# Low parts of one weight pair in four by an accumulating DMA, and pairs used one step later, in the feed-forward parts of a decoder layer

## The chip, the cores and the metric

The kernel runs on one core of a Trainium2 chip. The metric is device time in microseconds (us) for one execution. The engines are named as the profile names them: PE multiplies matrices (PEld is its weight load), DVE works on vectors, ACT on activations and copies, POOL is the general-purpose engine, which also issues DMAs whose descriptors software makes, and SP issues the weight loads. All of them run their own instruction queues in order and wait for each other by semaphores.

## What is computed

One hybrid decoder layer on `x` of 256 rows by 2048 columns, float32: a half-step SwiGLU feed-forward part with layer norm, a mixer (differential attention beside an RWKV-7 recurrence, with layer norm), and a second half-step feed-forward part with layer norm.

```python
def swiglu(x, w_gate, w_up, w_down):
    return (jax.nn.silu(x @ w_gate) * (x @ w_up)) @ w_down

x = layer_norm(alpha * x + 0.5 * swiglu(x, ffn1_w_gate, ffn1_w_up, ffn1_w_down), ln1_g, ln1_b)
p = x @ w_in
...                                   # attention and RWKV-7 on the columns of p
x = layer_norm(alpha * x + concat(o_attn, o_rwkv) @ w_out, ln2_g, ln2_b)
x = layer_norm(alpha * x + 0.5 * swiglu(x, ffn2_w_gate, ffn2_w_up, ffn2_w_down), ln3_g, ln3_b)
```

`D_MODEL` is 2048 and `D_FF` 5632, so each feed-forward part multiplies the 256 rows by two 2048x5632 matrices and one 5632x2048 matrix.

## The kernel before

**Three products for one.** PE multiplies in a rounded float32 form (`fp32r`). To keep float32 accuracy, each operand is split into a rounded high part and a low part, which is the original minus the high part. A product is then high x high, plus high x low, plus low x high: lines 113, 114 and 115. The names say which part an operand is: `wh` and `wl` for weights, `xh` and `xl` for the layer's input, `hh` (both parts) for the hidden activations.

**The weight stream.** All big products go through one object, `Stream`. Its method `block` runs over one block of up to 512 output columns and takes the inner dimension in pairs of 128-row tiles. One pair is one step, counted by `self.step` through the whole kernel. A step does this:

1. SP issues the load of 512 KB from HBM into a tile `raw` (line 134). There are three `raw` buffers (`NRAW`).
2. ACT copies `raw` into `wh`, which rounds it (line 137).
3. DVE subtracts `wh` from `raw` into `wl` (line 138).
4. `mm` issues the six matmuls of the pair for the first 128 rows of `x` (`tt` 0).
5. The pair is put on the list `pend`. Once that holds more than `LAG` pairs, the oldest one has its six matmuls for the second 128 rows (`tt` 1), and its `wh` and `wl` buffers are given back when those are done.

In a feed-forward part there are seven buffers for `wh` and `wl` (`NW`), taken in turn by `self.slot`, and `LAG` is 4: the pair of step s is used for the first rows in step s and for the second rows in step s + 4. In the mixer these are five and 2.

**The feed-forward part.** `ffn` runs in two halves of 6 and 5 blocks of hidden columns. For each block it runs a gate block and an up block of 8 steps each, then ACT takes the silu (line 222), DVE multiplies (line 227), PE transposes (line 230), and ACT and DVE split the result into two parts (lines 240 and 241). Then four down blocks of 12 or 10 steps add into `y`. A feed-forward part thus has 264 steps; the mixer has 136, so the first part is steps 1 to 264 and the second 401 to 664. At the end of each part `ln_tail` makes the layer norm, first for the first 128 rows, then for the second ones (lines 185 to 196), and `flush` issues the second-row matmuls that are still on `pend`.

**What else is on the queues.** POOL does a one-column copy ahead of each reload of the residual (line 262), one small operation of each layer norm (line 189), and the DMAs of the gains and biases (lines 207 and 208) and of the mixer's small tables (lines 289 to 319). ACT issues the DMAs of the residual. A planner of the framework orders each engine's instructions and places the waits; the `raw` tiles and the PSUM tiles are handed out from pools by it.

Of the kernel before, what the change touches and what calls it, by code (L numbers as in the profile page):

```python
# [10 lines left out]
F32 = mybir.dt.float32  # L11
F32R = mybir.dt.float32r
AF = mybir.ActivationFunctionType
ALU = mybir.AluOpType
AX = mybir.AxisListType

P = 128
# [10 lines left out]
LAMBDA_INIT = 0.8 - 0.6 * math.exp(-0.3 * 0)  # L28
LDEC = math.exp(-0.5)
SCALE = 64 ** -0.5  # L30
LAG = {"ffn": 4, "mix": 2}
NW = {"ffn": 7, "mix": 5}
NRAW = 3
BANKS = {"tr": ("at", 2), "sm": ("sm", 2), "pr": ("pr", 1), "at": ("at", 2)}
# [4 lines left out]
def build(tc, A, out):  # L39
# [15 lines left out]
    def nm(s):  # L55
        uid[0] += 1
        return f"{s}_{uid[0]}"

    V, SC, G, T = nc.vector, nc.scalar, nc.gpsimd, nc.tensor
# [29 lines left out]
    class Stream:  # L89
        def __init__(self):  # L90
            self.pend = []
            self.acc = {}
            self.bg = []
            self.credit = {}
            self.hooks = {}
            self.step = 0
            self.slot = 0
# [21 lines left out]
        def block(self, src, c0, w, ks, lhs, done):  # L119
            blk = dict(ks=ks, w=w, lhs=lhs, done=done)  # L120
            for ki in range(0, len(ks), 2):
                for f in self.hooks.get(self.step, ()):
                    f()
                self.step += 1
                n = 2
                r0 = ks[ki][0]
                raw = wp.tile([P, n, NB], F32, tag="raw", name=nm("raw"), bufs=NRAW)
                pool = wp if self.slot < NW["mix"] else self.pool
                wh, wl = (pool.tile([P, n, NB], F32R, tag=f"{t}{self.slot}", name=nm(t)) for t in ("wh", "wl"))
                self.slot = (self.slot + 1) % NW[self.name]  # L130
                g = 1 if self.step == 1 else n
                for k in range(0, n, g):
                    c = slice(k, k + g)
                    nc.sync.dma_start(out=raw[:, c, :w], in_=src[(r0 + k) * P:(r0 + k + g) * P, c0:c0 + w].rearrange("(k p) n -> p k n", p=P))
                for k in range(0, n, g):
                    c = slice(k, k + g)
                    SC.copy(out=wh[:, c, :w], in_=raw[:, c, :w])  # L137
                    V.tensor_tensor(out=wl[:, c, :w], in0=raw[:, c, :w], in1=wh[:, c, :w].bitcast(F32), op=ALU.subtract)  # L138
                st = (blk, ki, n, wh, wl)
                self.mm(st, 0)  # L140
                self.pend.append(st)
                if len(self.pend) > max(0, min(LAG[self.name], self.step // 4 - 1)):
                    self.mm(self.pend.pop(0), 1)
                self.run_bg()

        def flush(self):
            while self.pend:
                self.mm(self.pend.pop(0), 1)

# [813 lines left out]
```

## Time and profile before

| | |
|---|---|
| time, median of 2 runs (lowest, highest) | 2006.34 us (2005.94, 2006.73) |
| span of the profiled execution, first to last instruction | 2006.8 us |
| instructions | 24924 |
| PE busy | 1972.1 us, 98% of the span |
| weight loads of PE busy | 1618.6 us, 81% |
| DVE busy | 1145.7 us, 57% |
| ACT busy | 885.0 us, 44% |
| POOL busy | 34.2 us, 2% |
| moved by DMA | 373.35 MB, 186 GB/s on average |

The profiled execution is one of its own; its span stands within 0.05% of both timed runs. An engine's busy time is the union of its instructions, so a matmul row of 0.39 us overlaps the next one, since matmuls are pipelined. In a row of the order of time stand the start, the duration, engine, line, operation, output and input, and in brackets how long the engine had been idle and what ended that. In a row of the costliest groups stand busy time and mean duration in ns, and then the idle time before. In a row of the waits stand the total wait, the number and the longest.

### The profile page before, as it was taken

The numbers are of one execution on the slowest core, as the hardware profiler recorded it, in microseconds if no ns is written. First come the engines' busy times: TensorE is split into PE (matmuls) and PEld (weight loads), VectorE is DVE, ScalarE is ACT, GpSimd is POOL, SyncE is SP. The second block draws the span as 40 slices with busy tenths as digits, with TensorE's granted clock in tenths as the row PEclk, the third lists the DMA queues.
The fourth block names the chain that finished last, engine by engine and source line by source line (L and its number), as shares of the span: only waits on it lengthen the run. The fifth ranks groups of instructions, "written<-read, shape, count | busy, mean of one in ns | idle before, by whom it ended". The sixth has DMA issues, their size and how long they took to land.

```text
span 2006.8 us, 24924 instructions
## 1 busy us (share of the span) xinstructions
PE 1972.1 (98%) x9671; PEld 1618.6 (81%) x9671; DVE 1145.7 (57%) x1419; ACT 885.0 (44%) x1096; POOL 34.2 (2%) x68
## 2 busy tenths in 40 slices
PE   9999999999999999999999989999999999999997
PEld 7888888888888878878778777788888888888886
DVE  5555554445545566776668777745554544454555
ACT  5444443344444335645565444444444334444432
POOL 0200000000000000000000010000000000000000
PEclk9999999999999999999999989899999999999999
DMA  7766666667666656555445635666666666766663
GB/s 243 220 188 189 187 191 206 211 192 230 190 188 189 195 167 192 155 160 171 137 123 147 187 117 171 210 200 189 189 188 190 206 211 191 230 190 188 190 195 128
DMA packets 202008, 373.35 MB, mean 186 GB/s; under 512 B 22826, under 2 KB 24944, under 8 KB 201120
## 3 DMA queue, kind: packets, MB, share of 16 engines
q1 hardware_dynamic: 182928, 350.53, 57.8%
q10 hardware_dynamic: 17440, 14.29, 2.5%
q0 software_dynamic: 1520, 6.93, 1.0%
q8 instruction: 76, 1.25, 0.3%
q14 instruction: 44, 0.36, 0.0%
HBM read 364.10 MB, written 7.60 MB: 185 GB/s over the span
## 4 chain that ended last, share of the span: by engine, by line
PE 91%; DVE 4%; DMA 2%; ACT 1%; issue 1%; ACTq 0%; POOL 0%; DVEq 0%
PE acc L113 28%; PE acc L115 28%; PE acc L114 28%; DVE wl L138 1%; DMA raw<-in_ffn_w_gate_dram 1%; PE tr L230 1%; ACT wh L137 1%; DVE y L193 1%; DVE y L194 1%; PE sm L556 0%; PE tr L353 0%; DMA raw<-in_ffn_w_up_dram 0%; PE pr L498 0%; PE at L775 0%; PE tr L75 0%
## 5 line engine op out<-in xcount | busy, mean ns | idle before, releaser
L138 DVE TENSOR_TENSOR wl<-raw,wh 128x1024 fp32r<-128x1024 f32 (+1 forms) x665 | 807.9, 1217 | 649.1 <-ACT wh L137 648.4
L137 ACT CAST wh<-raw 128x1024 fp32r<-128x1024 f32 (+1 forms) x665 | 694.9, 1047 | 832.7 <-PE acc L115 728.3
L115 PE MATMUL acc<-wh,xl 128*128 128x512 f32 (+1 forms) x1952 | 740.6, 391 | 0.5 <-DVE xl L82 0.5
L114 PE MATMUL acc<-wl,xh 128*128 128x512 f32 (+1 forms) x1952 | 735.4, 392 | 3.9 <-DVE wl L138 3.9
L113 PE MATMUL acc<-wh,xh 128*128 128x512 f32 (+1 forms) x1952 | 728.1, 392 | 0.3 <-ACT xh L81 0.2
L114 PEld LDWEIGHTS acc<-wl,xh 128*128 128x128 f32 x1952 | 368.0, 189 | 80.0 <-DVE wl L138 5.2
L113 PEld LDWEIGHTS acc<-wh,xh 128*128 128x128 f32 x1952 | 368.2, 189 | 79.1 <-issue 3.0
L115 PEld LDWEIGHTS acc<-wh,xl 128*128 128x128 f32 x1952 | 367.8, 188 | 77.0 <-issue 2.3
L115 PE MATMUL acc<-wh,hh 128*128 128x512 f32 x704 | 254.5, 390 | 0.0
L114 PE MATMUL acc<-wl,hh 128*128 128x512 f32 x704 | 253.6, 389 | 0.0
L113 PE MATMUL acc<-wh,hh 128*128 128x512 f32 x704 | 252.6, 389 | 0.0
L114 PEld LDWEIGHTS acc<-wl,hh 128*128 128x128 f32 x704 | 132.1, 188 | 27.6
L115 PEld LDWEIGHTS acc<-wh,hh 128*128 128x128 f32 x704 | 132.2, 188 | 27.4
L113 PEld LDWEIGHTS acc<-wh,hh 128*128 128x128 f32 x704 | 132.1, 188 | 27.4
L241 DVE TENSOR_TENSOR hh<-tr,hh 128x512 fp32r<-128x512 f32 x44 | 30.4, 691 | 64.2 <-ACT hh L240 64.2
L240 ACT CAST hh<-tr 128x512 fp32r<-128x512 f32 x44 | 25.8, 586 | 91.2 <-PE tr L230 91.2
L227 DVE SCALAR_TENSOR_TENSOR h<-sg,acc 128x512 f32<-128x512 f32 x44 | 30.2, 687 | 34.9 <-PE acc L115 34.9
L222 ACT ACTIVATE sg<-acc 128x512 f32<-128x512 f32 x44 | 26.3, 598 | 42.9 <-PE acc L115 42.9
L230 PEld LDWEIGHTS tr<-ident,h 128*128 128x128 f32 x176 | 21.7, 140 | 6.3 <-DVE h L227 0.7
L230 PE MATMUL tr<-ident,h 128*128 128x128 f32 x176 | 26.4, 272 | 0.3 <-DVE h L227 0.3
L584 DVE TENSOR_TENSOR itmp<-U,Y 64x31 f32<-64x31 f32 (+15 forms) x62 | 20.5, 331 | 7.3 <-DMA U<-dU 5.9
L586 DVE TENSOR_TENSOR Y<-Y,itmp 64x31 f32<-64x31 f32 (+15 forms) x62 | 20.6, 332 | 1.4
(239 smaller groups left out, 746.8 us busy)
## 6 DMA issues: line engine op xcount, KB each, us to landing
raw<-in_ffn_w_up_dram SPq DMA_DIRECT2D x176, 512.0 KB, 3.8
raw<-in_ffn_w_down_dram SPq DMA_DIRECT2D x176, 512.0 KB, 4.2
raw<-in_ffn_w_gate_dram SPq DMA_DIRECT2D x175, 512.0 KB, 3.9
raw<-in_w_in_dram SPq DMA_DIRECT2D x96, 512.0 KB, 3.7
raw<-in_w_out_dram SPq DMA_DIRECT2D x32, 512.0 KB, 4.2
xs<-y ACTq DMA_DIRECT2D x16, 256.0 KB, 3.1
rc<-xs ACTq DMA_DIRECT2D x16, 256.0 KB, 4.3
lng<-in_ln_g_dram POOLq DMA_DIRECT2D x3, 1024.0 KB, 6.5
```

Source lines behind the costliest of these rows:

```text
L113: T.matmul(a, hi, wh[:, j, :w], start=(ki + j == 0), stop=False)
L114: T.matmul(a, hi, wl[:, j, :w], start=False, stop=False)
L115: T.matmul(a, lo, wh[:, j, :w], start=False, stop=(ki + j == last))
L137: SC.copy(out=wh[:, c, :w], in_=raw[:, c, :w])
L138: V.tensor_tensor(out=wl[:, c, :w], in0=raw[:, c, :w], in1=wh[:, c, :w].bitcast(F32), op=ALU.subtract)
L222: SC.activation(out=s, in_=acc, func=AF.Silu)
L227: V.scalar_tensor_tensor(out=h, in0=sg[tt], scalar=0.5, in1=acc, op0=ALU.mult, op1=ALU.mult)
L230: T.transpose(tr[:, i, :], h[:, i * P:(i + 1) * P], ident)
L240: SC.copy(out=hi, in_=tr)
L241: V.tensor_tensor(out=lo, in0=tr, in1=hi.bitcast(F32), op=ALU.subtract)
L584: V.tensor_tensor(out=tv, in0=U[:, 0:j, j:j + 1].to_broadcast([64, j, 32 - j]), in1=Y[:, j:j + 1, j:32].to_broadcast([64, j, 32 - j]), op= ...
L586: V.tensor_tensor(out=Y[:, 0:j, j:32], in0=Y[:, 0:j, j:32], in1=tv, op=ALU.add)
```

## The change

For the steps of a feed-forward part after step 16, those whose number leaves the remainder 3 or 7 modulo 8 get their low part in another way: ACT writes the negated, rounded tile into `wl` (an activation `Copy` with scale -1), and then a DMA issued by POOL adds the raw tile onto it in place. At remainder 3 the DMA reads the weights from HBM a second time, at remainder 7 it reads the `raw` tile in SBUF. The other steps keep the subtraction on DVE.

In the same steps a pair is kept back on a list `held` for one step, so that its matmuls for the first rows are issued after the next pair's conversions have been; `LAG` for the feed-forward part goes from 4 to 3. `flush` and the steps that don't hold pairs empty the list first.

```diff
-LAG = {"ffn": 4, "mix": 2}
+LAG = {"ffn": 3, "mix": 2}
...
             self.pend = []
+            self.held = []
...
                     SC.copy(out=wh[:, c, :w], in_=raw[:, c, :w])
-                    V.tensor_tensor(out=wl[:, c, :w], in0=raw[:, c, :w], in1=wh[:, c, :w].bitcast(F32), op=ALU.subtract)
+                    src_c = src[(r0 + k) * P:(r0 + k + g) * P, c0:c0 + w].rearrange("(k p) n -> p k n", p=P)
+                    how = self.step % 8 if self.name == "ffn" and self.step > 16 else 0
+                    if how in (3, 7):
+                        SC.activation(out=wl[:, c, :w], in_=raw[:, c, :w], func=AF.Copy, scale=-1.0)
+                        G.dma_start(out=wl[:, c, :w], in_=src_c if how == 3 else raw[:, c, :w], accum_op=ALU.add)
+                    else:
+                        V.tensor_tensor(out=wl[:, c, :w], in0=raw[:, c, :w], in1=wh[:, c, :w].bitcast(F32), op=ALU.subtract)
                 st = (blk, ki, n, wh, wl)
+                if self.name == "ffn" and self.step > 16:
+                    self.held.append(st)
+                    if len(self.held) < 2:
+                        continue
+                    st = self.held.pop(0)
+                else:
+                    self.unhold()
                 self.mm(st, 0)
...
+        def unhold(self):
+            while self.held:
+                st = self.held.pop(0)
+                self.mm(st, 0)
+                self.pend.append(st)
+
         def flush(self):
+            self.unhold()
             while self.pend:
                 self.mm(self.pend.pop(0), 1)
```

## The prediction, made before the change was run

> **What bounds the kernel now.** I read the head of the page first, then busy time by stretch, then the waits, then the order of time inside one feed-forward (FFN) stretch. "Step" is one weight pair (two 128x512 tiles).
>
> ```profile
> span 2006.8 us, 24924 instructions
> PE 1972.1 (98%) x9671; PEld 1618.6 (81%) x9671; DVE 1145.7 (57%) x1419; ACT 885.0 (44%) x1096; POOL 34.2 (2%) x68
> ...
> 58.00:735.00 677.00, 677.00 (x3029) 560.31 (x3027) 342.54 (x316) 279.77 (x288) 13.44 (x32) 1.00 0.65 197
> 735.00:760.00 25.00, 20.30 (x115) 18.05 (x114) 23.33 (x41) 9.79 (x16) 2.04 (x2) 0.86 0.52 165
> 1235.00:1275.00 40.00, 36.17 (x156) 28.83 (x155) 36.49 (x53) 13.32 (x17) 2.00 (x2) 0.87 0.61 191
> 1275.00:1985.00 710.00, 710.00 (x3175) 587.62 (x3174) 360.46 (x323) 295.48 (x304) 2.82 (x12) 1.00 0.65 196
> 1985.00:2006.00 21.00, 9.85 (x44) 7.83 (x42) 14.13 (x24) 0.00 (x0) 2.01 (x2) 0.86 0.30 101
> ```
>
> The columns of a stretch are its length, then busy time of PE, weight loads, DVE, ACT, POOL, then granted clock, DMA share and GB/s. In the two FFN stretches (677 and 710 us) PE is busy for all of it, at clock 1.00. The whole span leaves 2006.8 - 1972.1 = 34.7 us without PE, none of it in these two.
>
> Is that busy time PE's own pace, or something that slows it? The order of time answers:
>
> ```profile
> 404.39 1.05 ACT L137 CAST wh<-raw 128x1024 fp32r<-128x1024 f32 x1 [1.67 <-PE acc L115]
> 407.11 1.05 ACT L137 CAST wh<-raw 128x1024 fp32r<-128x1024 f32 x1 [1.67 <-PE acc L115]
> ...
> 420.71 1.05 ACT L137 CAST wh<-raw 128x1024 fp32r<-128x1024 f32 x1 [1.67 <-PE acc L115]
> ```
> ```profile
> 405.47 1.23 DVE L138 TENSOR_TENSOR wl<-raw,wh 128x1024 fp32r<-128x1024 f32 x1 [0.56 <-ACT wh L137]
> 408.19 1.22 DVE L138 TENSOR_TENSOR wl<-raw,wh 128x1024 fp32r<-128x1024 f32 x1 [1.49 <-ACT wh L137]
> ```
> ```profile
> 404.64 0.39 PE L114 MATMUL acc<-wl,hh 128*128 128x512 f32 x1
> 404.87 0.39 PE L115 MATMUL acc<-wh,hh 128*128 128x512 f32 x1
> 405.09 0.39 PE L113 MATMUL acc<-wh,hh 128*128 128x512 f32 x1
> 405.32 0.39 PE L114 MATMUL acc<-wl,hh 128*128 128x512 f32 x1
> 405.55 0.39 PE L114 MATMUL acc<-wl,xh 128*128 128x512 f32 x1
> 405.77 0.39 PE L115 MATMUL acc<-wh,xl 128*128 128x512 f32 x1
> ```
>
> A step takes (420.71 - 404.39) / 6 = 2.72 us; with 12 matmuls that is 0.227 us each. Matmul starts stand 0.22 to 0.23 us apart while ACT alone works (404.64 to 405.32) and while DVE does (405.55 to 405.77), so easing DVE can't quicken them. ACT idles 1.67 us before each conversion, and what ends the wait is PE giving back a weight buffer: the feed waits for PE.
>
> ```profile
> ACT wh L137 <- PE acc L115: 728.3, 472, 8.2
> ...
> PEld acc L114 <- DVE wl L138: 5.2, 4, 2.5
> ...
> PE acc L114 <- DVE wl L138: 3.9, 3, 2.2
> ```
> ```profile
> SPq L134 <- DVE wl L138: 1451.2, 594, 29.8
> ```
>
> PE waited for a low part 5.2 and 3.9 us in the whole run. SP, which issues the loads, waits for line 138 to give back a raw buffer. **So nothing in the FFNs can be gained; the question is whether the new chain still fits.**
>
> **The change part by part.**
>
> *Counting.* Steps 17 to 264 (first FFN) and 401 to 664 (second; the mixer has 136 steps) are concerned. Remainders 3 and 7 modulo 8 occur 31 times each in the first and 33 in the second: 128 pairs, in 64 periods of 8 steps (21.8 us each).
>
> *Removed:* 128 subtractions of 1.22 us = 156 us of DVE. Off the path by the waits above: worth nothing.
>
> *Added on ACT:* 128 negated copies. The trace has none; the nearest row is line 137, same engine and shape, 1.05 us (134 us in all, ACT 885 to about 1,020). The activation of line 222 against the cast of line 240, both 512 wide, bounds the form:
>
> ```profile
> L240 ACT CAST hh<-tr 128x512 fp32r<-128x512 f32 x44 | 25.8, 586 | 91.2 <-PE tr L230 91.2
> ...
> L222 ACT ACTIVATE sg<-acc 128x512 f32<-128x512 f32 x44 | 26.3, 598 | 42.9 <-PE acc L115 42.9
> ```
>
> 12 ns in 586, so 1.05 to 1.08. Behind it on ACT stands the next conversion, which has 1.67 us of idle time; that hides it once, with 1.05 us of ACT per 2.72 us step.
>
> *Added on POOL and the DMA engines:* 128 accumulating DMAs of 512 KB. No row shows one. The nearest:
>
> ```profile
> q1 hardware_dynamic: 182928, 350.53, 57.8%
> ...
> raw<-in_ffn_w_up_dram SPq DMA_DIRECT2D x176, 512.0 KB, 3.8
> ...
> lng<-in_ln_g_dram POOLq DMA_DIRECT2D x3, 1024.0 KB, 6.5
> lnb<-in_ln_b_dram POOLq DMA_DIRECT2D x3, 1024.0 KB, 9.1
> ```
> ```profile
> 454.48 0.53 POOL L207 DMA_DIRECT2D lng<-in_ln_g_dram  x1 [0.20 <-POOL lnb L206]
> ```
>
> 350.53 MB take 57.8% of 2006.8 us, so 302 GB/s while busy, and 512 KB (0.524 MB) is 1.74 us of all 16 engines. A plain load lands in 3.8 us, so about 2.06 us of it is fixed. An accumulation must read its destination as well as its source: 2.06 + 2 x 1.74 = 5.5 us alone, 7.3 with one load interleaved. The layer-norm gain, 1 MB on the same software queue beside the loads, took 6.5. I take L = 6.4 us from issue to landing, near that row. Bounds: 3.8 (costs as a load) and 9.1 (the second of two such transfers). The DMA engines have room: 8 loads and 2 accumulations are 14 + 7 = 21 of 21.8 us at the busy rate, tight but below one.
>
> The Trainium skill weighs against this number. "DMA: Bandwidth & Descriptors", section "Anatomy of one DMA — SWDGE (gpsimd) path", gives 2.0 us plus bytes over 436 GB/s; its price for the gain's 1 MB is 4.4 us, the row says 6.5, so I keep the row. "Collectives: The Full Stack", section "The bandwidth ceiling: the fold count and why AG ≠ RS ≠ AR", says an adding DMA costs its second source read and not the add; no run here shows it yet. By the formula with two reads L would be 4.4 and the change would be hidden.
>
> *Used one later, lag 3 instead of 4.* Let T = 2.72 and 0 be the moment a weight buffer comes free. Before, the pair is needed 2T = 5.4 us later, and casting plus subtracting takes 1.05 + 1.23 + gaps = 2.4. After, the second half of the rows still runs at the same place (held 1 + lag 3), so the buffer frees at the same place, but the first use is at 3T = 8.16, the low part at about 8.4 (second matmul). Ordinary pairs gain cover. An accumulated pair needs 1.05 + 1.05 + 0.15 (gaps) + L = 2.25 + L = 8.65: late by **0.25 us**.
>
> *Raw buffers, the larger term.* There are three. For remainder 7 the source is the raw tile itself, so it is held to the landing at 8.65 instead of 2.4. I assume that the pool hands on the buffer that is free first: the load three steps on takes the next pair's buffer (free at 5.1), the one four steps on, itself an accumulated pair (remainder 3), takes the held one. SP issues in order, so later loads queue behind it. It is issued at 8.75, lands at 12.55 instead of 10.9, is cast and negated by 14.75, and its low part lands 14.85 + 6.4 = 21.25. PE wants it at 7T + 0.23 = 19.3, plus the first 0.25: late by **1.7**. Together 1.9 us a period (2L - 10.9 in general); the remainder-3 pair gives its raw tile back after the negation, so the chain recovers before the next period.
>
> 64 x 1.9 = **122 us**.
>
> *One-offs.* In the flush, the held pair's first half now runs after one second half fewer, 6 matmuls = 1.4 us less PE work to hide the first rows' layer norm. At the end DVE goes from it to the second rows' without a gap:
>
> ```profile
> 1992.59 2.73 DVE L194 SCALAR_TENSOR_TENSOR y<-y,rs,lnb 128x512 f32<-128x512 f32 x4
> 1995.24 0.68 DVE L266 TENSOR_TENSOR y<-y,acc 128x512 f32<-128x512 f32 x1
> ```
>
> so +1.4 us there and +1.4 at the first FFN's end. Gains, biases and the mixer's small tables go through the same POOL queue; an accumulation behind one gain and bias (9.1 us for both) is some 3 us later still, twice: about 6. On the other side at most the 4.7 + 3.8 us that PE idles in the two layer-norm stretches could go; I count nothing. Sum of one-offs: about +8.
>
> 122 + 8 = 130 on 2006.8, the profiled span, which is the median of the timed runs (2006.34) within 0.03%: **2135 us**.
>
> **The rivals.**
>
> *Hidden (not slower).* L of 5.4 or less makes 2L - 10.9 negative: the one-step hold covers the accumulation, and only the one-offs stay, 2007 + 3 to 8, about **2013**. For it: 5.5 us alone, and PE's order, in which first-half and second-half matmuls (hh at 405.32, xh at 405.55) are interleaved, so a planner that foresees a late low part may put other matmuls ahead. Against: the 6.5 us row, taken under just these loads. Also 65% of the DMA time in these stretches is already taken. The formula of the Trainium skill's DMA page, 4.4 us by the section named above, speaks for this rival, and the same row against it.
>
> *Strict rotation.* If the load three steps on waits for the held buffer itself, the next load is issued right behind it and lands 1.5 us later: 2L - 9.4 = 3.4 us a period, 218 + 8: **2233**. The pool's order isn't visible in the trace, where subtractions release in order either way.
>
> *The accumulation is slow.* At L = 8 to 9.1 a period loses 5.1 to 7.3 us: **2340 to 2480**, and stalls so long would cost clock too (0.86 in the stretches with layer norms). It decides from about twice the 3.8 us of a load.
>
> **How the numbers follow.** Forecast (stall of 1 to 2.5 us a period, 2080 to 2175) 0.38; hidden 0.34; rotation 0.16; slow accumulation 0.11; faster by more than 2% (40 us, which is also about what a measurement of this kernel can tell from no change) 0.01, since PE without work is only 34.7 us in all. The range reaches from hidden, 2003, to above rotation, 2310, and leaves out most of the slow case. Within 2% takes hidden whole: 0.34; slower 0.65.
>
> **What would show it.** In the profile after: PE waiting for a DMA on the low part at line 114 for 100 us or more; the accumulating issues landing near 6.4 us; SP waiting for the same DMAs; DVE down by 156 us, ACT up by 134. The forecast is wrong if they land under 5.5 us, or over 8, or if SP's raw loads get slower than 4.5 us beside them, and if the FFN stretches stay at full PE busy time.

## The result, and the profile after

The changed kernel takes **2252.62 us** (median of 2 runs, 2245.59 to 2259.65) against 2006.34: a ratio of 1.1226, interval 1.1143 to 1.1309. The forecast was 2135, the range 2003 to 2310. The profiled execution took 2245.59, its span is 2243.8.

Head of the page after, its queues, three groups, and its DMA issues (the last column is us to landing), with some lines between left out:

```profile
span 2243.8 us, 25241 instructions
PE 2044.5 (91%) x9671; PEld 1650.6 (74%) x9671; DVE 986.9 (44%) x1291; ACT 1003.5 (45%) x1224; POOL 169.8 (8%) x196
...
q1 hardware_dynamic: 182928, 350.53, 48.9%
q0 software_dynamic: 28144, 74.04, 17.3%
...
L142 ACT ACTIVATE wl<-raw 128x1024 fp32r<-128x1024 f32 x128 | 135.8, 1061 | 189.6 <-PE acc L115 156.8
L143 POOL DMA_DIRECT2D wl<-raw x64 | 58.2, 910 | 728.4 <-ACT wl L142 727.6
L143 POOL DMA_DIRECT2D wl<-in_ffn_w_gate_dram x21 | 25.6, 1218 | 304.5 <-ACT wl L142 304.5
...
raw<-in_ffn_w_up_dram SPq DMA_DIRECT2D x176, 512.0 KB, 4.6
raw<-in_ffn_w_down_dram SPq DMA_DIRECT2D x176, 512.0 KB, 5.0
wl<-raw POOLq DMA_DIRECT2D x64, 512.0 KB, 4.6
wl<-in_ffn_w_down_dram POOLq DMA_DIRECT2D x22, 512.0 KB, 9.7
wl<-in_ffn_w_gate_dram POOLq DMA_DIRECT2D x21, 512.0 KB, 8.9
```

The span grew by 237 us. PE without work went from 34.7 to 2243.8 - 2044.5 = 199.3 us (+164.6), PE busy time from 1972.1 to 2044.5 (+72.4). The landings fall into two kinds in this kernel: 4.6 us where the source is the raw tile in SBUF, 9 to 10 us where it is HBM. SP's own loads of the FFN weights are slower too, 3.8 to 4.6 us for `up`.

Granted clock over the run, from the view of the cores; first the kernel before, then after:

```profile
core 0: 2006.8 us, clock 0.990
```
```profile
core 0: 2243.8 us, clock 0.963
```

2243.8 x 0.037 = 83 us against 2006.8 x 0.010 = 20. So about 63 of the 72 us of extra busy time are clock, not work.

Busy time by stretch after (columns as in the prediction), of most of the two FFNs:

```profile
58.00:700.00 642.00, 583.74 (x2483) 471.90 (x2483) 216.06 (x204) 279.56 (x292) 66.26 (x82) 0.96 0.76 214
1450.00:2200.00 750.00, 678.93 (x2884) 549.68 (x2883) 253.36 (x235) 320.40 (x332) 64.13 (x68) 0.96 0.74 210
```

Before, PE was busy for every microsecond of the FFN stretches, at clock 1.00. Now it lacks 58 of 642 and 71 of 750 us, at 0.96. What it waits for, from the waits after (total us, times, longest), and below them a row of SP's own waits:

```profile
PE acc L115 <- DMA wl<-in_ffn_w_down_dram: 67.6, 22, 5.6
...
PE acc L115 <- DMA wl<-in_ffn_w_up_dram: 43.4, 20, 3.3
PE acc L115 <- DMA wl<-in_ffn_w_gate_dram: 39.0, 18, 4.5
```
```profile
SPq L135 <- DMA wl<-raw: 402.4, 61, 10.2
```

(Line 115 is the low-part matmul, line 114 before.) These three rows are 150.0 us in 60 waits, 2.5 us each, all for a pair whose accumulation reads HBM (remainder 3; there are 64 periods). For an accumulation from the raw tile PE waited 1.3 us in the whole run, in two waits. Yet SP waited 402 us for just those. The chain of work that ended last, in order of time (start, us; short pieces left out), shows how one becomes the other:

```profile
1620.91 4.72 DMA wl<-raw
1625.69 0.37 SPq L135
1626.17 4.73 DMA raw<-in_ffn_w_gate_dram
1631.00 1.07 ACT wl L142
...
1632.52 9.49 DMA wl<-in_ffn_w_gate_dram
1642.06 0.50 PE acc L115
...
1643.61 0.43 PE acc L114
```

The remainder-7 accumulation lands at 1625.63; only then does SP issue the next two loads. The second is the remainder-3 pair's: landed at 1630.90, negated, accumulated from HBM, and PE starts the moment that lands. Its idle time then is 2.55 us:

```profile
1642.06 0.50 PE L115 MATMUL acc<-wl,xh 128*128 128x512 f32 x1 [2.55 <-DMA wl<-in_ffn_w_gate_dram]
```

Afterwards, from 1643.6 to 1646.4, a matmul takes 0.43 us instead of 0.23. Two stretches around it, columns as above (the granted clock is the third from the end):

```profile
1632.00:1642.00 10.00, 7.50 (x35) 5.86 (x34) 3.74 (x4) 3.77 (x6) 1.21 (x1) 1.00 0.87 237
...
1644.00:1647.00 3.00, 3.00 (x10) 2.35 (x9) 0.92 (x2) 1.22 (x2) 0.00 (x0) 0.56 0.49 138
```

### The profile page after: what moved, and what is told of

It reads as the page before. It is cut to its first block, busy times and chain, and to the rows that moved or that the text cites. A ratio compares the mean times of both kernels' runs of the same rounds, so it can differ in the third digit from the quotient of the medians.

```text
span 2243.8 us, 25241 instructions
## 1 busy us (share of the span) xinstructions
PE 2044.5 (91%) x9671; PEld 1650.6 (74%) x9671; DVE 986.9 (44%) x1291; ACT 1003.5 (45%) x1224; POOL 169.8 (8%) x196
## 3 DMA queue, kind: packets, MB, share of 16 engines
q1 hardware_dynamic: 182928, 350.53, 48.9%
q0 software_dynamic: 28144, 74.04, 17.3%
## 5 line engine op out<-in xcount | busy, mean ns | idle before, releaser
L145 DVE TENSOR_TENSOR wl<-raw,wh 128x1024 fp32r<-128x1024 f32 (+2 forms) x537 | 651.2, 1215 | 1058.1 <-ACT wh L138 1057.6
L115 PE MATMUL acc<-wl,xh 128*128 128x512 f32 (+1 forms) x1952 | 776.2, 401 | 87.2 <-DMA wl<-in_ffn_w_up_dram 43.4
L114 PE MATMUL acc<-wh,xh 128*128 128x512 f32 (+1 forms) x1952 | 764.8, 399 | 12.7 <-ACT xh L81 9.8
L116 PE MATMUL acc<-wh,xl 128*128 128x512 f32 (+1 forms) x1952 | 770.3, 399 | 0.5 <-DVE xl L82 0.5
L115 PE MATMUL acc<-wl,hh 128*128 128x512 f32 x704 | 283.4, 406 | 67.6 <-DMA wl<-in_ffn_w_down_dram 67.6
L116 PE MATMUL acc<-wh,hh 128*128 128x512 f32 x704 | 280.0, 405 | 0.0
L114 PE MATMUL acc<-wh,hh 128*128 128x512 f32 x704 | 276.0, 400 | 0.0
L142 ACT ACTIVATE wl<-raw 128x1024 fp32r<-128x1024 f32 x128 | 135.8, 1061 | 189.6 <-PE acc L115 156.8
L143 POOL DMA_DIRECT2D wl<-raw x64 | 58.2, 910 | 728.4 <-ACT wl L142 727.6
L143 POOL DMA_DIRECT2D wl<-in_ffn_w_gate_dram x21 | 25.6, 1218 | 304.5 <-ACT wl L142 304.5
L143 POOL DMA_DIRECT2D wl<-in_ffn_w_down_dram x22 | 26.6, 1210 | 204.5 <-ACT wl L142 203.1
```

Source lines behind the costliest of these rows:

```text
L114: T.matmul(a, hi, wh[:, j, :w], start=(ki + j == 0), stop=False)
L115: T.matmul(a, hi, wl[:, j, :w], start=False, stop=False)
L116: T.matmul(a, lo, wh[:, j, :w], start=False, stop=(ki + j == last))
L142: SC.activation(out=wl[:, c, :w], in_=raw[:, c, :w], func=AF.Copy, scale=-1.0)
L143: G.dma_start(out=wl[:, c, :w], in_=src_c if how == 3 else raw[:, c, :w], accum_op=ALU.add)
```

## The experiments

Edits are against the changed kernel unless said. Ratios are to the kernel before in the same session (2007.1 to 2009.0 us there).

### No accumulation, only the later use

```diff
-                    if how in (3, 7):
+                    if how in ():
```

> Pairs used one later and lag 3, but every low part by the subtraction: no negated copy, no accumulating DMA. Two theories of the 237 us that the changed kernel lost. HOLD: the raw tile that the remainder-7 DMA keeps delays the load for the remainder-3 pair, and that delay is most of the loss. LANDING: the DMA that reads HBM lands 8.9 to 9.7 us after its issue (4.6 for the one that reads SBUF), which is more than the cover by itself. Both expect 2007 + 1.4 + 1.4 for the shorter flush, 2008 to 2010. Over 2030 would mean that the order of use itself costs time, and both would be short of a cause.

**2022.56 us, 1.0076 (1.0059 to 1.0093)**: a miss, some 15 us rather than a few. The stretches of this kernel, and of the kernel before below them:

```profile
58.00:735.00 677.00, 677.00 (x3027) 560.28 (x3027) 340.66 (x316) 280.61 (x287) 13.24 (x32) 1.00 0.65 196
735.00:1290.00 555.00, 527.63 (x3210) 423.07 (x3209) 400.89 (x724) 282.54 (x474) 15.27 (x16) 0.97 0.52 155
```
```profile
735.00:1275.00 540.00, 522.12 (x3194) 419.85 (x3193) 396.50 (x721) 280.74 (x473) 15.27 (x16) 0.97 0.53 158
```

The first FFN is as full of PE work as before. The loss lies in the stretch behind it, where PE lacks 27.4 us instead of 17.9. So the later use costs nothing where it acts, and something at its end.

### The later use in the second FFN alone

```diff
-                    if how in (3, 7):
+                    if how in ():
...
-                if self.name == "ffn" and self.step > 16:
+                if self.name == "ffn" and self.step > 400:
...
-                if len(self.pend) > max(0, min(LAG[self.name], self.step // 4 - 1)):
+                if len(self.pend) > max(0, min(LAG[self.name] + (self.name == "ffn" and self.step <= 400), self.step // 4 - 1)):
```

> Pairs used one later and lag 3 in the second feed-forward part alone, no accumulation. The run with both parts so took 15 us more than the kernel before, with PE busy for all of the two feed-forward stretches. If that comes from the first part's end, through another order in the mixer behind it: 2007 to 2011 here. If the order of use costs in each part: 2013 to 2017.

**2010.2 us, 1.0011 (1.0001 to 1.0021).**

The middle stretch is again that of before: PE works 521.64 of its 540 us, after 522.12. The 15 us hang on the first FFN's end and on how the mixer's work is planned behind it; which instruction there is late wasn't traced further.

### One of the two accumulations alone

Remainder 3, from HBM:

```diff
-                    if how in (3, 7):
+                    if how == 3:
```

> Only remainder 3 (HBM source) is accumulated, 64 pairs; remainder 7 by the subtraction, so no raw tile is held. LANDING: 2.25 + 9.4 us against 8.4 us of cover is 3.3 us late, 64 times: 209 us, with slow clock behind the waits up to 250: 2200 to 2260. HOLD: without the late load at most a third of the loss is left: under 2090.

**2147.99 us, 1.0700 (1.0669 to 1.0731)**, between what the two theories had. From its waits, then its DMA issues:

```profile
PE acc L115 <- DMA wl<-in_ffn_w_down_dram: 52.2, 22, 3.1
```
```profile
wl<-in_ffn_w_down_dram POOLq DMA_DIRECT2D x22, 512.0 KB, 10.0
```

Here no raw tile is held for a DMA, and the low part is still late, by 52.2 / 22 = 2.4 us for `down`. By the prediction's schedule 2.25 + 10.0 against a cover of 8.4 is 3.9. So the remainder-3 accumulations alone carry 2148 - 2023 = 125 us over the run without accumulation.

Remainder 7, from the raw tile (`if how == 7:`):

> Only remainder 7 (SBUF source) is accumulated, 64 pairs; remainder 3 by the subtraction. Both theories: 2.25 + 4.6 = 6.9 us is under the cover of 8.4, and the late loads behind the held raw tile hit only pairs with 2.7 us more cover than before the change: 2008 to 2025. The hold itself still shows as SP waiting for the DMA, about 400 us in all.

**2058.0 us, 1.0251 (1.0229 to 1.0274)**, more than expected. SP's waits, then PE's:

```profile
SPq L135 <- DMA wl<-raw: 398.4, 62, 7.9
```
```profile
PE acc L115 <- DMA wl<-raw: 17.1, 18, 2.2
```

This DMA itself is seldom late for PE. SP waits for it as long as in the changed kernel (402.4), and these accumulations cost 35 us over the run without any. 2023 + 125 + 35 = 2183: the changed kernel has about 70 us more, which only both together produce.

### Both from the raw tile

```diff
-                        G.dma_start(out=wl[:, c, :w], in_=src_c if how == 3 else raw[:, c, :w], accum_op=ALU.add)
+                        G.dma_start(out=wl[:, c, :w], in_=raw[:, c, :w], accum_op=ALU.add)
```

> Both remainders are accumulated from the raw tile in SBUF, 128 pairs; nothing is read twice from HBM, and both tiles are held. LANDING: each lands in 4.6 us; a pair whose load was late is ready at 2.25 + 4.6 + 0.1 + 5.2 + 2.15 + 4.6 = 18.9 us against 19.3: 2010 to 2050. HOLD: two holds per period instead of one, so at least the loss of the changed kernel: 2240 or more.

**2275.02 us, 1.1332 (1.1310 to 1.1355).** The late landing of HBM is gone and nothing is won.

```profile
SPq L135 <- DMA wl<-raw: 738.4, 125, 8.2
```
```profile
PE acc L115 <- DMA wl<-raw: 177.9, 109, 4.5
```

With two held tiles in eight steps SP waits nearly twice as long. The median landing of 5.9 us is early enough by itself (2.25 + 5.9 = 8.15 against 8.4), and yet PE waits 109 times. The chain that ended last (short pieces left out) shows why: each accumulated pair's load goes out, behind one other, only when the accumulation of the pair four steps before it has landed.

```profile
1614.23 5.92 DMA wl<-raw
...
1620.66 4.50 DMA raw<-in_ffn_w_up_dram
...
1625.27 1.07 ACT wl L142
...
1626.68 5.84 DMA wl<-raw
```

From one issue to the next that is 12.45 us here and 12.9 us at the median of the run, for four steps that PE does in 4 x 2.72 = 10.9 us. Such a chain isn't late once; it sets the pace. 2.0 us too much, 126 times, is about 250 us, as much as the run lost over the one without accumulation (2275.0 - 2022.6 = 252). The next two runs give the held tile a buffer of its own.

### The accumulated pairs' raw tile in a buffer of its own

```diff
-                raw = wp.tile([P, n, NB], F32, tag="raw", name=nm("raw"), bufs=NRAW)
+                own = self.name == "ffn" and self.step > 16 and self.step % 4 == 3
+                raw = self.pool.tile([P, n, NB], F32, tag="rawx", name=nm("raw"), bufs=1) if own else wp.tile([P, n, NB], F32, tag="raw", name=nm("raw"), bufs=NRAW)
```

In the changed kernel:

> The changed kernel with a fourth raw buffer: the accumulated pairs have one of their own, so no other pair's load waits for an accumulating DMA. HOLD: SP's 402 us of waiting for the DMA on wl goes to nearly nothing, the remainder-3 pair's load is in time, and what is left is its own late landing, as where only the HBM pairs were accumulated (2148): 2130 to 2165. LANDING as the whole cause: no change, 2240 to 2260.

**2182.79 us, 1.0868 (1.0843 to 1.0893)**: 70 us less than the changed kernel, and the 2183 that the single parts add up to; the run was expected lower still, at 2130 to 2165. Its waits of PE, and below them SP's for the accumulation from the raw tile:

```profile
PE acc L115 <- DMA wl<-in_ffn_w_down_dram: 39.7, 22, 2.7
PE acc L115 <- DMA wl<-in_ffn_w_gate_dram: 38.7, 17, 8.6
...
PE acc L115 <- DMA wl<-in_ffn_w_up_dram: 19.1, 12, 2.9
```
```profile
SPq L136 <- DMA wl<-raw: 459.1, 61, 10.2
```

PE waited 97.5 us for the HBM landings instead of 150.0. SP's wait was expected to go to nearly nothing and didn't: the next accumulated pair's load still waits for the buffer. So the length of SP's wait is no measure of its price. What went away is the delay of the load three steps on, and with it the queueing behind that load: the accumulated pair's load is issued 0.05 us behind the landing instead of 0.51 and takes 3.95 us instead of 4.74 (medians). Matmul starts stand 0.227 us apart as before, so the added tile itself cost no pace.

Together with both from the raw tile:

> Both remainders accumulated from SBUF, with the fourth raw buffer for them: 128 accumulations of 512 KB, none of which holds a buffer that another pair's load wants. HOLD: 2.25 + 4.6 to 5.9 us against a cover of 8.4, and loads in time: back to the kernel that only uses pairs one later (2023), 2020 to 2045. CONTENTION (the accumulations slow the loads and each other by their traffic, whatever they hold): most of the 2275 of the same kernel with three raw buffers stays, over 2150.

**2070.76 us, 1.0306 (1.0289 to 1.0324)**: 204 us less than with three shared buffers, from the buffer alone, though not the 2020 to 2045 expected. So where both accumulations hold their raw tile, sharing its buffer with other loads makes most of the loss, 204 of 252 us. SP's wait for the accumulations is again no shorter (951.3 us, after 738.4), but the chain from issue to issue is: 5.5 us of landing, 0.05, 3.9 of load, 0.1 and 1.4 (medians) are 10.95 us, about the 10.9 that PE needs. 48 us over the run without accumulation remain. ACT's waits for the negation in this run:

```profile
ACT wl L143 <- DMA raw<-in_ffn_w_down_dram: 130.1, 37, 5.1
```

A negation that waits on ACT for its tile holds up the conversions behind it (the timeline of the second scratch run, further down, has such a case), and a chain with no slack passes every delay on. Which of the two makes the 48 us isn't shown.

### More cover for the HBM landing

```diff
-LAG = {"ffn": 3, "mix": 2}
+LAG = {"ffn": 2, "mix": 2}
...
-                    if how in (3, 7):
+                    if how == 3:
...
-                    if len(self.held) < 2:
+                    if len(self.held) < 3:
```

> Only the HBM pairs accumulated (2148 with pairs used one later), now with pairs used two later and lag 2, so 2.7 us more cover: 11.1 us. LATE LANDING as the cause of that run's loss: 2.25 + 8 to 10 us is 10.3 to 12.3, at most 1.1 us late for the down blocks and nothing for the others: 2025 to 2060. If the slower loads beside the accumulation are the cause, the added cover helps little: over 2110.

**2038.47 us, 1.0146 (1.0125 to 1.0167)**, as expected of a late landing: 110 us less than the same accumulations with one step of cover. Its DMA issues and waits:

```profile
wl<-in_ffn_w_down_dram POOLq DMA_DIRECT2D x22, 512.0 KB, 9.9
```
```profile
PE acc L115 <- DMA wl<-in_ffn_w_down_dram: 6.0, 12, 0.9
```

The DMA takes as long as before (9.9 against 10.0 us), the bytes are the same, and PE's waits for it all but vanish. It was the lack of cover in the schedule, not the accumulations' traffic, that cost most of the time there.

### Accumulations that nobody waits for

All 128 read HBM into a scratch tile whose values are thrown away; every low part comes from the subtraction.

```diff
-                        SC.activation(out=wl[:, c, :w], in_=raw[:, c, :w], func=AF.Copy, scale=-1.0)
-                        G.dma_start(out=wl[:, c, :w], in_=src_c if how == 3 else raw[:, c, :w], accum_op=ALU.add)
-                    else:
+                        sc = self.pool.tile([P, n, NB], F32R, tag="sc2", name=nm("sc2"), bufs=1)
+                        SC.activation(out=sc[:, c, :w], in_=raw[:, c, :w], func=AF.Copy, scale=-1.0)
+                        G.dma_start(out=sc[:, c, :w], in_=src_c, accum_op=ALU.add)
+                    if True:
```

> All 128 negated copies and accumulating DMAs, all with the HBM source, but into a scratch tile that nobody reads; every low part by the subtraction, no raw tile held. The computation is whole, the accumulated values are thrown away. WAITS as the cause (late landing, held buffers): the traffic, the ACT and POOL work alone cost little: 2023 (pairs one later) to 2050. CONTENTION: the loads are slowed, ACT waits for them and PE for ACT: over 2100.

**2202.03 us, 1.0964 (1.0942 to 1.0986).** By number this is contention's, but the trace doesn't settle it: ACT waited 628.5 us for loads ahead of its conversions, and 221.5 us for loads ahead of the scratch negations, a wait that the run was to be free of. With the own raw buffer added:

> As the run whose 128 accumulations go into scratch (2202), with the fourth raw buffer of its own for every fourth pair. The accumulated values are thrown away, the low parts come from the subtraction. RING (three raw buffers: a load that lands in 5.8 to 6.2 us instead of 4, plus 2.4 to 3.5 us of use, is 8.2 to 9.7 us for three steps, 2.7 to 3.2 us a step against PE's 2.72): four buffers give 2.1 to 2.4 us a step, and the time falls to 2023 to 2060 though the traffic is the same. BANDWIDTH (the DMA engines themselves are the bound): no change, 2180 to 2210.

**2183.4 us, 1.0868 (1.0846 to 1.0889)**: nearly nothing won, by number BANDWIDTH's. One of its waits on ACT, then three pieces of its timeline:

```profile
ACT sc L144 <- DMA raw<-in_ffn_w_down_dram: 289.0, 44, 9.0
```
```profile
501.50 1.06 ACT L144 ACTIVATE sc<-raw 128x1024 fp32r<-128x1024 f32 x1 [7.76 <-DMA raw<-in_ffn_w_gate_dram]
502.46 1.03 ACT L139 CAST wh<-raw 128x1024 fp32r<-128x1024 f32 x1
...
503.88 2.95 ACT L139 CAST wh<-raw 128x1024 fp32r<-128x1024 f32 x3
```

The order of work puts the negation, which nobody needs, ahead of conversions that PE needs: ACT stands 7.76 us for a later load, and then does four conversions without a gap but for a short cast. Both runs are inconclusive on contention. They do show the loads beside 128 HBM accumulations, `up` in 5.8 us in the first of them after 4.6 in the changed kernel. And they show how fast an accumulation from HBM can land, in the first run:

```profile
sc<-in_ffn_w_down_dram POOLq DMA_DIRECT2D x44, 512.0 KB, 6.1
```

`gate` and `up` took 5.9 and 5.8 us. That is the same size, source and form as the 9 to 10 us of the changed kernel. What differs is what runs beside it. When POOL's issue ended, two or more of SP's loads were under way in 60 of the 64 HBM accumulations of the changed kernel, and at most one in 249 of these two runs' 256 (counted from the issues and landings in the traces). The seven others took 6.9 to 11.9 us. The accumulations from the raw tile keep to this in the run that has them alone: 5.6 us at the median beside one load, 7.0 beside two. The count isn't the whole rule: with both from the raw tile and the own buffer, 104 stood beside two loads and took 5.5.

### Rows of 2 KB instead of 4 KB, and a control for them

The raw tile gets 8 more columns, so that a transfer out of it has 256 rows of 2 KB instead of 128 of 4 KB; remainder 7 alone is accumulated.

```diff
-                raw = wp.tile([P, n, NB], F32, tag="raw", name=nm("raw"), bufs=NRAW)
+                raw = wp.tile([P, n, NB + 8], F32, tag="raw", name=nm("raw"), bufs=NRAW)
...
-                    if how in (3, 7):
+                    if how == 7:
```

> As the run that accumulates remainder 7 alone from SBUF (2058), with raw tiles padded by 8 columns a row, so that the DMA moves 256 rows of 2 KB as the HBM one does, and not 128 of 4 KB. If the long landing of the HBM pairs comes from the number of rows (descriptors made by POOL's software), POOL's instruction goes from 0.91 to 1.2 us, the landing from 5.8 to 8 or more, and the time over 2100. If it comes from HBM as the source, the landing stays under 6.5 and the time at 2050 to 2070.

**2081.87 us, 1.0366 (1.0345 to 1.0386).** Its accumulations' landing:

```profile
wl<-raw POOLq DMA_DIRECT2D x64, 512.0 KB, 5.6
```

The issue on POOL takes 1.20 us, as in the HBM form (0.87 with 4 KB rows), and the landing is no longer than with those (5.8). So the number of rows goes with POOL's time, and does not explain the 9 to 10 us from HBM. The run's time, between what the two guesses had, carries something else, which the control isolates: the kernel before, with the same 8 columns added and nothing else.

> The kernel before with raw tiles padded by 8 columns a row and nothing else. The run that did this to the remainder-7 pairs had matmul starts 0.233 us apart instead of 0.227 at full clock. If the shifted place of the weight tiles does that: 7968 matmuls x 6 ns is 48 us, 2050 to 2060 here. If it came from the accumulation: 2006 to 2010.

**2052.34 us, 1.0222 (1.0205 to 1.0240)**, without a single accumulation. The timeline's conversions, as in the prediction:

```profile
403.05 1.05 ACT L137 CAST wh<-raw 128x1024 fp32r<-128x1024 f32 x1 [1.75 <-PE acc L115]
...
422.61 1.05 ACT L137 CAST wh<-raw 128x1024 fp32r<-128x1024 f32 x1 [1.75 <-PE acc L115]
```

Seven steps in 19.56 us are 2.79 a step, against 2.72: 0.233 us a matmul instead of 0.227, with ACT still waiting for PE. The padding makes the rows of `raw` longer and changes where the tiles lie; which of the two slows PE isn't shown.

None of these runs beats the kernel before. In its FFNs PE is busy for the whole stretch, and nothing that the accumulation takes off DVE was on the path.

## Why the prediction was right, and where it was not

The direction and the cause that was named hold: PE waits for late low parts, by way of the accumulations' landing and of the raw buffer. The measured 2252.62 us lies in the range, but past the 2080 to 2175 of the forecast itself and nearest to the rival of strict rotation.

**The bound: right.** DVE fell by 158.8 us (1145.7 to 986.9; predicted 156) and that bought nothing: with PE always busy in the FFNs there was nothing to buy. ACT rose by 118.5 (predicted 134); the negation itself takes 135.8 us, 1.061 each and inside the 1.05 to 1.08 worked out, and ACT's other lines came out 17 us shorter.

**The landing, L = 6.4: mis-sized, by being one number.** From the raw tile it is 4.6 us in the changed kernel, from HBM 8.9 to 9.7 there. The first is under the 5.5 and the second over the 8 named as signs of a wrong forecast, and 9.7 lies past the upper bound of 9.1. Both signs cost the sum something different. Remainder 7: 2.25 + 4.6 = 6.85 against 8.4, late for PE by 1.3 us in the whole run, where 0.25 us a period was predicted. Remainder 3: late even with its raw tile on time, as the run with HBM alone shows, where no more than 0.25 was predicted without the held buffer. The two numbers aren't prices of the two sources: in the scratch runs the same DMA from HBM landed in 5.8 to 6.1 us. They go with how many of SP's loads are under way beside it, which the forecast's row, the layer-norm gain, has in one mixture only.

**Engine time: two reads, nearly right.** The software queue's share gives 17.3% x 2243.8 = 388 us, less about 20 for the 6.93 MB it moved before (`q0` in the run without accumulation is the same 6.93 MB at 1.0%):

```profile
q0 software_dynamic: 1520, 6.93, 1.0%
```

368 / 128 = 2.9 us of all 16 engines for each, against 48.9% x 2243.8 x 0.524 / 350.53 = 1.64 for a load: 1.75 times. "Collectives: The Full Stack" of the Trainium skill (section "The bandwidth ceiling: the fold count and why AG ≠ RS ≠ AR") puts an adding DMA's price in its second source read; these rows are close to that. With two reads, the formula of the Trainium skill's "DMA: Bandwidth & Descriptors" (section "Anatomy of one DMA — SWDGE (gpsimd) path") gives an estimate of 4.4 us. The landings of 4.6 us are near it; those of 5.8 to 6.1 from HBM in the scratch runs are a third longer, and those of 8 to 10 twice as long. The formula itself has no term for other traffic.

**The raw buffer: the mechanism right, the pool's order wrong.** The step "I assume that the pool hands on the buffer that is free first" failed. The load three steps on waits for the held buffer, as in the rival of strict rotation, and the next is issued 0.48 us behind it (1625.69, 1626.17); it starts within 0.3 us of the landing in 55 of 63 periods. The term itself is confirmed by an own buffer, which takes away the shared wait: 70 us in the changed kernel, 204 where both kinds come from the raw tile. The chain of the changed kernel, quoted with the result, tests its sizes: from the issue of one accumulation to the landing of the next the forecast had 21.25 - 2.25 = 19.0 us, the trace has 1642.01 - 1620.91 = 21.1. The parts differ more than the sum: 4.72 instead of 6.4 from SBUF, 9.49 instead of 6.4 from HBM, and 4.73 for a load instead of 3.8. Two errors of L cancelled for the most part.

**Loss per period:** 1.9 us predicted, 2.5 measured in 60 of 64 (150 us against 122). The rotation rival had 3.4 and 2233, the total nearest to what was measured. It is near partly by luck: its 3.4 is 0.9 us a period too much, 58 us in all, and stands in for the 63 us of clock that it doesn't hold.

**Clock: left out.** The sum charged it only to the rival of slow accumulation. Waits of 2.5 us were enough, and some 63 us followed: the largest term that the sum lacks. The record of the clock has 39 stretches at half rate in the changed kernel, 30 of them of 3.41 us, and 5 before. At "TensorE: Matmul & The Clock Gate" (section "What's actually happening") the Trainium skill gives half rate after an idle window of about 3.4 us. The half rate is in the trace, 0.43 us for 0.23, and lasts some 3 us; but PE's gap ahead of it was 2.55 us, and the clock in the 10 us that hold this gap is 1.00, so here a gap shorter than that window was enough. One of 1.83 us, at 88 us, was enough too, and one of 2.89, at 242 us, was followed by none: not every wait is charged.

**One-offs:** +8 predicted. The later use alone costs 15, at the first FFN's end and in the mixer's planned work; the two flush terms of 1.4 us are within that, and not separated.

**Loads beside the accumulations:** 4.6 to 5.0 us, past the 4.5 named as a sign. What of the loss goes by this contention rather than by the order of waits stays open: the two runs made for it brought in a wait of their own. Nor do the loads slow down wherever there are accumulations: beside the 64 from HBM alone they landed in 3.8 to 4.1 us, as before the change, and beside the 64 from the raw tile alone in 4.5 to 4.8. The run with more cover is the nearest to a price: against the run without accumulation, whose pairs are used one step later and not two, its 64 HBM accumulations cost 2038.5 - 2022.6 = 16 us, contention and all else together.

In all: before 2006, the later use 15, remainder 3 alone 125 (110 of it gone with one more step of cover), remainder 7 alone 35, the two meeting 70 (gone with an own buffer), with the clock inside these numbers. That sums to 2251. The division is one of runs, not of the trace, and holds for this order of adding.

## What to carry to other kernels

- An engine that is relieved is worth only what waits for it. Where the bound engine is busy for a whole stretch, look at what the new path holds and for how long: a buffer read by a slow DMA delays the loads behind it, in the queue's order, and the late item can be another than the one that was changed. Where held buffers follow one another, add up the closed chain and set it against the pace of the bound engine.
- Price a new DMA by its place: ask what else is on the DMA engines when it is issued, and take one landing for each such place; check how a pool rotates before assuming that it hands on the first free buffer; and try cover (one more step of delay) before taking traffic away, since it separates late from too much.
- Charge short, repeated waits of PE twice, once for the wait and once for the clock that may follow.

## What the hardware showed that was not expected

- An accumulating DMA of 512 KB landed in 4.6 to 5.9 us from SBUF, and from HBM in 8 to 10 us in the changed kernel and the runs near it, but in 5.8 to 6.1 us in the scratch runs. Its time of the 16 engines is much the same from both sources (software queue 9.4% of 2059.5 us with 64 of the one kind alone, 9.5% of 2141.2 with 64 of the other). Rows of 2 KB from SBUF landed in 5.6 us, so the size of the rows isn't the cause, and the source alone isn't either; the landings go with SP's loads under way at the issue. Whether the DMA stands behind these or shares the engines with them stays open.

- Padding the rows of `raw` by 8 columns slowed matmuls from 0.227 to 0.233 us with nothing else changed (2052.34 against 2009.04 us), though no matmul reads `raw`. An experiment that changes a tile's size needs a control with the size alone.
